# Splitting mixer weights ahead into DRAM, and moving scaling, halves and centring between engines, in a two-layer hybrid trunk

## Chip, cores and metric

One core of a Trainium2 chip runs the kernel. The metric is the device time of one execution in microseconds; lower is better. TensorE (PE in the profile) does the matmuls, VectorE (DVE), ScalarE (ACT) and GpSimd (POOL) the rest; SyncE (SP) issues the transfers. Inputs are float32, and the kernel works in float32 throughout, with products split in two parts as described below.

## What is computed

```python
def reference(x, ...):
    for layer in range(DEPTH):                       # 2 layers
        x = x + 0.5 * swiglu_ffn(x, ffn1_norm[layer], ffn1_w_in[layer], ffn1_w_out[layer])
        if layer % 2 == 0:
            x = x + retention_dilated_mixer(x, mix_norm[layer], hyb_w_in[e], ret_gn[e], hyb_w_out[e])
        else:
            x = x + stick_breaking_mixer(x, mix_norm[layer], sb_w_in[o], sb_w_out[o])
        x = x + 0.5 * swiglu_ffn(x, ffn2_norm[layer], ffn2_w_in[layer], ffn2_w_out[layer])
    return rms_norm(x, final_norm)
```

The sequence has 512 tokens, the model 1024 columns, the channel mixing 2816. `swiglu_ffn` is `(silu(h @ gate) * (h @ up)) @ w_out` on the RMS-normed `h`. The first mixer has 8 heads of 64 with retention (scores times a decay, a group norm per head, a swish gate) and 8 heads of dilated attention (a masked softmax). The second has 16 heads of stick-breaking attention: with z the score of a query and an earlier key, the weight is `exp(log_sigmoid(z) + sum over later keys of log_sigmoid(-z))`.

## The kernel before

Activations lie transposed: 8 chunks of 128 model columns by 512 tokens (`x`, and `hh` after the norm). Each float32 operand of a large product is split into a part `hi` (a rounded copy) and a part `lo` (the rest, by a subtract), and `mm3` (L138) sums three matmuls, hi by hi, hi by lo and lo by hi. `weight` (L121) does this for a weight tile of 128 by up to 1024: a load by SyncE into one of four `wraw` slots, `hi` by a ScalarE copy (L128) into `whi`, `lo` by a subtract (L129) into `wlo`, two slots each. The engine of L129 is in `lo_eng`: VectorE during the channel mixing, GpSimd during the two mixers (`lo_eng[0] = nc.gpsimd` at the foot of `trunk`).

The program runs in this order: `ffn` and `out_ffn` of layer 0, `hybrid`, `ffn` and `out_ffn` again, the same pair of layer 1, `stick`, `ffn` and `out_last`. `ffn` has 22 steps of two projection tiles (gate and up), each 8 chunks by three matmuls of 128 by 512. `out_ffn` has 8 steps of 66 matmuls.

`hybrid` first makes four gates (weights `hyb_g`). Then it works through eight pairs of heads, four of retention and four of dilated attention; `prep` of the next pair stands ahead of the core of the present one. `prep` projects values (`hyb_rv` or `hyb_dv`), then q and k through `qk_rot`: a shuffle (L441), three VectorE operations of the rotation (L443 to L445), and `pack_q` (ScalarE copies L399 and L400, VectorE rest L401) or `pack_k` (VectorE copy L381 and rest L382, twice each on 64 partitions). `retention_core` multiplies scores by the decay (L470), splits them (L146, L147), multiplies by the values (`attend`, L420, L425), then norms per head: a matmul with `bd` gives the mean (L477), VectorE subtracts it (L478), ScalarE squares (L480), a second matmul gives the variance (L482), and VectorE scales (L484, L486). `dilated_core` takes the mask and the minimum of each block of scores (L508), the exponents on ScalarE, a reciprocal (L511) and a scaling (L512) for each of the eight blocks, then transposes (L519) and goes on as above.

`stick_core` works on eight pairs, each head in three banks: scores, Abs (L593), Exp and Ln on ScalarE, L596 on VectorE, a split into `sp` (L151 and L152), the sums over later keys by matmuls with `tri` and `nones` (L617), an exponent, and a split into `ah`. `split_v` (L149) makes `hi` by a VectorE copy (L151) and `lo` by a subtract (L152) on the engine it is given: GpSimd for a pair's output, VectorE elsewhere. `out_mix` projects the eight outputs (`oa`, `ob` weights).

The program is written in this order, and a scheduler then sets each engine's own order by when buffers and operands come free; SyncE issues a load when its `wraw` slot is free. PSUM has eight banks: `acc` 3, `att` 4, `po` 1.

Of the kernel before, what the change touches and what calls it, by code (L numbers as in the profile page):

```python
# [34 lines left out]
def trunk(ctx: ExitStack, tc: tile.TileContext, a: dict, out: bass.AP):  # L35
# [113 lines left out]
    def split_v(hi, lo, src, eng=None):  # L149

        nc.vector.tensor_copy(out=hi, in_=src)  # L151
        (eng or nc.vector).tensor_tensor(out=lo, in0=src, in1=f32(hi), op=ALU.subtract)  # L152
# [223 lines left out]
    def pack_k(y):  # L376

        t = B((P, 2, SEQ), F32R, "qk")
        for e in range(2):
# [1 line left out]
            nc.vector.tensor_copy(out=t[own, e, :], in_=y[own, :])  # L381
# [113 lines left out]
    def dilated_core(p, q, k, v, dmask, outs):  # L495
        rows = {}
        for b in BANKS:
            ps = ATT()
# [4 lines left out]
            for e, i, at in QPARTS[b]:
                n = (i + 1) * P
                sl = slice(at, at + n)
                st = T((P, 4))

                nc.vector.tensor_tensor_reduce(out=s[:, sl], in0=ps[:, sl], in1=dmask[:, SEQ - n:], op0=ALU.add,  # L508
                                               op1=ALU.min, scale=1.0, scalar=3.0e38, accum_out=st[:, 0:1])
# [315 lines left out]
```

## Time and profile before

| | us |
|---|---|
| median of 3 runs | 2083.76 (2082.23 to 2086.93) |
| profiled execution, its own time | 2081.9 |
| its span | 2080.0 |
| mean granted TensorE clock | 0.992 of full speed |

| stage (part of the span, us) | TensorE busy | VectorE | ScalarE | GpSimd |
|---|---|---|---|---|
| channel mixing, 800 to 900 | 100.00 | 45.35 | 29.38 | 0.00 |
| hybrid, 360 to 700 | 302.55 of 340 | 251.40 | 150.93 | 104.63 |
| stick-breaking, 1400 to 1720 | 294.02 of 320 | 246.02 | 181.54 | 87.32 |

The first row is from a window of 100 us in a channel-mixing stage; the others contain the mixer and some of what stands beside it. An engine's time is busy time, which includes time in which an operation is under way and waits for something in it. The granted clock is that of TensorE. In the group rows the last column is the idle time ahead of a group on its engine, with what ended it; in the timeline rows it stands in brackets.

### The profile page before, as it was taken

To read this page: it belongs to the slowest core of one execution; us is meant where nothing else is said; L and a number is where in the kernel's file an instruction comes from. 1 tells how busy PE (TensorE), PEld (TensorE's weight loads), DVE (VectorE), ACT (ScalarE), POOL (GpSimd) and SP (SyncE) were. 2 spreads that over 40 slices of the span, in tenths; PEclk is the share of its full clock that TensorE was granted. 3 is DMA by queue.
4 is the path that set the end of the run, shared out by engine and by line. 5 is a ranking of instruction groups with operands and counts; after the bars stand their busy time and mean duration, and the time that the engine had idled before them with its cause. 6 is when DMAs were issued, how large, how long until landed. Compare 5 with 4: busy or idle time off the path is not lost.

```text
span 2080.0 us, 23646 instructions
## 1 busy us (share of the span) xinstructions
PE 1999.6 (96%) x9440; PEld 1662.7 (80%) x9440; DVE 1113.3 (54%) x1640; ACT 769.8 (37%) x1124; POOL 196.4 (9%) x104
## 2 busy tenths in 40 slices
PE   8999999987889999999999999999898999999997
PEld 7888888876667788888888888888777778888887
DVE  6444433378987644443344444336777874444334
ACT  5323332334445423233233323225655653232323
POOL 0000000532223000000000000003322220000000
PEclk9999999999999999999999999999999999999999
DMA  5223333312112332333332323332111032223333
GB/s 183 100 93 100 95 94 100 116 62 71 58 35 71 102 101 92 101 88 100 97 101 91 102 96 92 101 97 75 61 42 46 28 100 91 100 93 101 93 92 125
DMA packets 55695, 186.51 MB, mean 90 GB/s; under 512 B 6304, under 2 KB 7072, under 8 KB 55584
## 3 DMA queue, kind: packets, MB, share of 16 engines
q1 hardware_dynamic: 55584, 185.00, 28.0%
q8 instruction: 74, 1.21, 0.2%
q14 instruction: 37, 0.30, 0.0%
HBM read 182.88 MB, written 2.10 MB: 89 GB/s over the span
## 4 chain that ended last, share of the span: by engine, by line
PE 84%; DVE 12%; ACT 3%; issue 1%; DMA 0%; SPq 0%; DVEq 0%; ACTq 0%
PE acc L142 18%; PE acc L143 18%; PE acc L141 18%; PE att L141 8%; PE att L142 8%; PE att L143 8%; PE att L617 2%; PE po L420 2%; DVE qk L381 1%; ACT t L90 1%; DVE tp L444 1%; PE acc L345 1%; PE acc L344 1%; PE acc L343 1%; DVE qk L382 1%
## 5 line engine op out<-in xcount | busy, mean ns | idle before, releaser
L128 ACT CAST whi<-wraw 128x1024 fp32r<-128x1024 f32 (+3 forms) x352 | 356.3, 1012 | 1007.9 <-PE acc L142 550.4
L129 DVE TENSOR_TENSOR wlo<-wraw,whi 128x1024 fp32r<-128x1024 f32 (+1 forms) x276 | 328.5, 1190 | 238.9 <-ACT whi L128 236.9
L141 PE MATMUL acc<-h,whi 128*128 128x512 f32 x992 | 390.6, 394 | 6.0 <-ACT h L174 6.0
L142 PE MATMUL acc<-h,whi 128*128 128x512 f32 x992 | 389.8, 393 | 0.9 <-DVE h L175 0.6
L143 PE MATMUL acc<-h,wlo 128*128 128x512 f32 x992 | 390.0, 393 | 0.0
L129 POOL TENSOR_TENSOR wlo<-wraw,whi 128x1024 fp32r<-128x1024 f32 (+2 forms) x76 | 167.4, 2202 | 1436.6 <-ACT whi L128 1376.8
L141 PE MATMUL att<-h,whi 128*128 128x512 f32 x704 | 275.1, 391 | 0.0
L143 PE MATMUL att<-h,wlo 128*128 128x512 f32 x704 | 274.3, 390 | 0.0
L142 PE MATMUL att<-h,whi 128*128 128x512 f32 x704 | 273.9, 389 | 0.0
L141 PEld LDWEIGHTS acc<-h,whi 128*128 128x128 f32 x992 | 187.8, 189 | 44.9 <-ACT h L174 5.9
L142 PEld LDWEIGHTS acc<-h,whi 128*128 128x128 f32 x992 | 187.7, 189 | 41.1 <-DVE h L175 3.6
L143 PEld LDWEIGHTS acc<-h,wlo 128*128 128x128 f32 x992 | 187.6, 189 | 39.0 <-issue 0.7
L315 DVE TENSOR_TENSOR tp<-att,r 128x512 f32<-128x512 f32 x88 | 60.9, 692 | 281.4 <-PE att L143 281.4
L309 DVE TENSOR_TENSOR tp<-acc,r 128x512 f32<-128x512 f32 x88 | 60.9, 692 | 183.6 <-PE acc L143 183.4
L141 PEld LDWEIGHTS att<-h,whi 128*128 128x128 f32 x704 | 132.3, 188 | 28.0 <-issue 0.7
L142 PEld LDWEIGHTS att<-h,whi 128*128 128x128 f32 x704 | 132.0, 188 | 27.9 <-issue 0.7
L143 PEld LDWEIGHTS att<-h,wlo 128*128 128x128 f32 x704 | 132.1, 188 | 27.8 <-issue 0.2
L141 PE MATMUL acc<-o,whi 128*128 128x512 f32 (+1 forms) x352 | 135.3, 384 | 0.0
L142 PE MATMUL acc<-o,whi 128*128 128x512 f32 (+1 forms) x352 | 134.8, 383 | 0.0
L143 PE MATMUL acc<-o,wlo 128*128 128x512 f32 (+1 forms) x352 | 134.3, 382 | 0.0
L141 PEld LDWEIGHTS acc<-o,whi 128*128 128x128 f32 x352 | 66.5, 189 | 11.7
L142 PEld LDWEIGHTS acc<-o,whi 128*128 128x128 f32 x352 | 66.5, 189 | 11.7
(179 smaller groups left out, 2960.0 us busy)
## 6 DMA issues: line engine op xcount, KB each, us to landing
wraw<-f_in SPq DMA_DIRECT2D x174, 512.0 KB, 3.4
wraw<-f_out SPq DMA_DIRECT2D x68, 448.0 KB, 3.3
wraw<-f_out SPq DMA_DIRECT2D x34, 512.0 KB, 3.5
wraw<-sb_q SPq DMA_DIRECT2D x8, 512.0 KB, 3.4
wraw<-sb_k SPq DMA_DIRECT2D x8, 512.0 KB, 3.4
wraw<-sb_v SPq DMA_DIRECT2D x8, 512.0 KB, 3.4
wraw<-hyb_oa SPq DMA_DIRECT2D x8, 320.0 KB, 2.8
wraw<-sb_oa SPq DMA_DIRECT2D x8, 320.0 KB, 2.8
```

The source lines that it names most:

```text
L90: r = nc.scalar.activation(out=o, in_=i, func=f, **kw)
L128: nc.scalar.copy(out=hi[:, :cols], in_=raw[:, :cols])
L129: lo_eng[0].tensor_tensor(out=lo[:, :cols], in0=raw[:, :cols], in1=f32(hi[:, :cols]), op=ALU.subtract)
L141: nc.tensor.matmul(ps, h[:, col:col + P], rhs_hi, start=first, stop=False)
L142: nc.tensor.matmul(ps, h[:, col:col + P], rhs_lo, start=False, stop=False)
L143: nc.tensor.matmul(ps, l[:, col:col + P], rhs_hi, start=False, stop=last)
L309: nc.vector.tensor_mul(out=t1, in0=pg, in1=rr)
L315: nc.vector.tensor_mul(out=t2, in0=pu, in1=rr)
L343: nc.tensor.matmul(o, hi, wh, start=k == 0 and t % 2 == 0, stop=False, skip_group_check=True)
L344: nc.tensor.matmul(o, hi, wl, start=False, stop=False, skip_group_check=True)
L420: nc.tensor.matmul(po[:, SEQ - n:], st, banks[b][:, c, at:at + n], start=j == 0 and c == 0, stop=j == NB - 1 and c == 1, skip_group_check= ...
L617: nc.tensor.matmul(z[:, at + n - m:at + n], st, sp[:, c, s0:s0 + m], start=False, stop=i == len(adds) - 1 and c == 1, skip_group_check=True)
```

## The change

The weights of the mixers are split while a channel mixing runs and kept in DRAM. `cut_ahead` takes one unit (one weight tile) at a time: it calls `weight`, and writes `hi` and `lo` to a DRAM tile by two transfers. `ffn` calls it at the end of each step from the third on, `out_ffn` at the end of each step where it is given units. The hybrid mixer's 28 units of 1024 columns (`hyb_g`, values, q, k) are split in the first `ffn` (20) and `out_ffn` (8) of layer 0, the 36 stick-breaking units (with the output weights `sb_oa` and `sb_ob`) in the second `ffn` of layer 0 and the first of layer 1, 18 each. `weight_cut` later loads both halves: on odd turns one transfer of both into a `whl` slot, on even turns two transfers into two `wraw` slots. The hybrid mixer's output weights (`hyb_oa`, `hyb_ob`, 12 tiles) are still split where they are used, now by VectorE. `whi` and `wlo` (two slots each) become `whl` (three slots for both halves).

Besides, `pack_k`'s hi, the hi of the pairs' outputs and `r23`'s hi go from VectorE to ScalarE; the outputs' lo from GpSimd to VectorE. The group norm's first matmul takes `cd` (identity minus `bd`), so its result is already centred, and the subtract goes. The eight reciprocals per pair of dilated heads become two of 128 by 4, and the scaling goes to ScalarE, after all of a head's blocks. In `stick_core` the last loop takes the banks in the order bc, bb, ba.

```diff
-    whi = ctx.enter_context(tc.tile_pool(name="whi", bufs=2))
-    wlo = ctx.enter_context(tc.tile_pool(name="wlo", bufs=2))
+    whl = ctx.enter_context(tc.tile_pool(name="whl", bufs=3))
+    dram = ctx.enter_context(tc.tile_pool(name="dram", bufs=1, space=bass.MemoryType.DRAM))
...
+    def cut_ahead(key, cols):
+        src = a[key[0]]
+        for i in key[1:]:
+            src = src[i]
+        hi, lo = weight(src, cols)
+        keep = dram.tile([P, 2, cols], F32, tag="cut_" + "_".join(map(str, key)), name="cut_" + "_".join(map(str, key)))
+        for i, part in enumerate((hi, lo)):
+            nc.sync.dma_start(keep[:, i, :], f32(part[:, :cols]))
+        cut[key] = keep
+
+    def weight_cut(key, cols):
+        turns[0] += 1
+        keep = cut[key]
+        if turns[0] % 2:
+            hl = whl.tile([P, 2, 1024], F32R, tag="whl", name=nm("whl"))
+            nc.sync.dma_start(f32(hl[:, :, :cols]), keep)
+            return hl[:, 0, :], hl[:, 1, :]
+        hl = [wraw.tile([P, 1024], F32R, tag="wraw", name=nm("wcut")) for _ in range(2)]
+        for i in range(2):
+            nc.sync.dma_start(f32(hl[i][:, :cols]), keep[:, i, :])
+        return hl
+
+    def unit(key, cols):
+        if key in cut:
+            return weight_cut(key, cols)
...
     def out_ffn(w_out, us, gcol, ahead=None):
             norm_chunk(d, gcol, ss)
+            if ahead:
+                cut_ahead(*ahead.pop(0))
...
     def ffn(r, w_in, first=None, pieces=None, ahead=None):
             us.append(u)
+            if ahead and f > 1:
+                cut_ahead(*ahead.pop(0))
...
     def pack_k(y):
-            nc.vector.tensor_copy(out=t[own, e, :], in_=y[own, :])
+            nc.scalar.copy(out=t[own, e, :], in_=y[own, :])
...
     def retention_core(p, q, k, v, gate, outs, bd, cd):
-        mu = ATT()
-        nc.tensor.matmul(mu, bd, o, start=True, stop=True)
-        nc.vector.tensor_sub(out=o, in0=o, in1=mu)
+        cen = ATT()
+        nc.tensor.matmul(cen, cd, o, start=True, stop=True)
         sq = T()
-        nc.scalar.activation(out=sq, in_=o, func=AF.Square)
+        nc.scalar.activation(out=sq, in_=cen, func=AF.Square)
...
-        nc.vector.tensor_mul(out=o, in0=o, in1=rs)
+        nc.vector.tensor_mul(out=o, in0=cen, in1=rs)
-        split_v(oo[:, 0, :], oo[:, 1, :], o, nc.gpsimd)
+        split(oo[:, 0, :], oo[:, 1, :], o)
...
     def dilated_core(p, q, k, v, dmask, outs):
-                nc.vector.reciprocal(st[:, 2:3], st[:, 1:2])
-                nc.vector.tensor_scalar(s[:, sl], s[:, sl], st[:, 2:3], None, op0=ALU.mult)
+            if b[0] == "A":
+                nc.vector.reciprocal(st[:, 2, :], st[:, 1, :])
+                for i in range(NB):
+                    nc.scalar.activation(out=rows[e, i], in_=rows[e, i], func=AF.Copy, scale=st[:, 2, i:i + 1])
...
     def stick_core(p, q, k, v, cm, outs, idr, tri, nones):
-            split_v(r23[:, 0, :], r23[:, 1, :], t2, nc.vector)
+            split(r23[:, 0, :], r23[:, 1, :], t2)
-            for b in (bb, bc, ba):
+            for b in (bc, bb, ba):
...
-    lo_eng[0] = nc.gpsimd
     ss = hybrid(ss, 16)
-    lo_eng[0] = nc.vector
```

Three places show how instructions move. The first is SyncE's queue at the join of layer 0's first channel mixing and the hybrid mixer. Before, the last loads of the output projection are followed by the gates' weights and the tables:

```order
L127 DMA wraw_2458<-f_out 128x896
L127 DMA wraw_2492<-hyb_g 128x1024
...
L127 DMA wraw_2615<-hyb_g 128x1024
L450 DMA o_395_2651<-rot_ret 128x1024
L460 DMA o_435_2951<-decay 128x1024
```

Now there are the loads of the last units to be split, their writes (L150), and the loads of split weights (L161 both halves, L165 one half):

```order
L127 DMA wraw_2606<-f_out 128x896
L150 DMA cut_hyb_dq_2547<-whl_2543 128x1024 x2
L127 DMA wraw_2638<-hyb_dk 128x1024
L165 DMA wcut_2697<-cut_hyb_g_471 128x1024
...
L165 DMA wcut_2760<-cut_hyb_g_627 128x1024
L150 DMA cut_hyb_dk_2643<-whl_2639 128x1024 x2
...
L161 DMA whl_2647<-cut_hyb_g_393 128x2048
L161 DMA whl_2729<-cut_hyb_g_549 128x2048
```

The first gate's tile (`cut_hyb_g_393`) now stands behind the last unit's writes, and behind loads for the second and fourth gates.

The second place is a pair of the stick-breaking mixer, where k's projection (`acc`) has ended and the first scores (`att`) are to be turned into `sp`. VectorE before:

```order
L434 TENSOR_TENSOR tp_10457<-acc_10417,r_9851 128x512
L381 CAST qk_10459<-tp_10457 64x512 x2
L382 TENSOR_TENSOR qk_10459<-tp_10457,qk_10459 64x512 x2
L596 SCALAR_TENSOR_TENSOR t_10471<-att_10464,t_10471 128x512
L596 SCALAR_TENSOR_TENSOR t_10483<-att_10479,t_10483 128x256
L151 CAST sp_10476<-t_10471 128x512
```

VectorE now, at the same pair:

```order
L476 TENSOR_TENSOR tp_10588<-acc_10550,r_10006 128x512
L424 TENSOR_TENSOR qk_10590<-tp_10588,qk_10590 64x512 x2
L642 SCALAR_TENSOR_TENSOR t_10602<-att_10595,t_10602 128x512
L642 SCALAR_TENSOR_TENSOR t_10614<-att_10610,t_10614 128x256
L188 CAST sp_10607<-t_10602 128x512
```

The two copies of k have left VectorE. ScalarE before, from q's last copies on:

```order
L400 ACTIVATE qk_10450<-tp_10448 64x512
L128 CAST whi_10673<-wraw_10672 128x1024
L593 ACTIVATE t_10471<-att_10464 128x512
L593 ACTIVATE t_10483<-att_10479 128x256
L90 ACTIVATE t_10471<-t_10471 128x512
```

ScalarE now:

```order
L442 ACTIVATE qk_10581<-tp_10579 64x512
L423 CAST qk_10590<-tp_10588 64x512 x2
L639 ACTIVATE t_10602<-att_10595 128x512
L639 ACTIVATE t_10614<-att_10610 128x256
L90 ACTIVATE t_10602<-t_10602 128x512
```

A weight's copy has gone from the row, and k's two copies stand ahead of the Abs (L593, now L639).

The third place is ScalarE in a pair of dilated heads. Before, exponents (L90) alternate with the splits of transposed blocks, and the scaling between them is VectorE's:

```order
L90 ACTIVATE t_3980,t_3990<-t_3980,t_3990 128x128
L146 CAST ah_4018<-att_4013 128x512
L146 CAST c_663_4024<-att_4021 128x256
L90 ACTIVATE t_3996,t_3999<-t_3996,t_3999 128x256
L146 CAST ah_4032<-att_4027 128x512
L90 ACTIVATE t_4005,t_4008<-t_4005,t_4008 128x512
```

Now a head's four scalings (L558) stand between exponents, and the splits (L183) come later:

```order
L90 ACTIVATE t_4061,st_4062<-t_4061,st_4062 128x384
L558 ACTIVATE t_4033<-t_4033,st_4034 128x128
L558 ACTIVATE t_4044<-t_4044,st_4034 128x256
L558 ACTIVATE t_4033<-t_4033,st_4034 128x384
L558 ACTIVATE t_4050<-t_4050,st_4034 128x512
L90 ACTIVATE t_4061,st_4062<-t_4061,st_4062 128x128
L90 ACTIVATE t_4072,st_4062<-t_4072,st_4062 128x256
L90 ACTIVATE t_4078,st_4062<-t_4078,st_4062 128x512
L183 CAST ah_4093<-att_4088 128x512
```

The first head's scaling follows the second head's first exponent, and the split of the first transposed block waits behind all of the second head's exponents.

More of the change, by code (lines that the diff above doesn't have):

```diff
@@ L123, in weight @@
         raw = wraw.tile([P, 1024], F32, tag="wraw", name=nm("wraw"))
-        hi = whi.tile([P, 1024], F32R, tag="whi", name=nm("whi"))
-        lo = wlo.tile([P, 1024], F32R, tag="wlo", name=nm("wlo"))
+        hl = whl.tile([P, 2, 1024], F32R, tag="whl", name=nm("whl"))
+        hi, lo = hl[:, 0, :], hl[:, 1, :]
         if pieces is None:
@@ L137, in weight, with mm3 @@
         return hi, lo
-    def mm3(ps, whl, col, rhs_hi, rhs_lo, first, last):
-        h, l = whl
+    cut = {}
+    def cut_ahead(key, cols):
[7 more added lines that the diff above has]
+        cut[key] = keep
+    turns = [0]
+    def weight_cut(key, cols):
+        turns[0] += 1
+        keep = cut[key]
+        if turns[0] % 2:
+            hl = whl.tile([P, 2, 1024], F32R, tag="whl", name=nm("whl"))
+            nc.sync.dma_start(f32(hl[:, :, :cols]), keep)
[7 more added lines that the diff above has]
+            return weight_cut(key, cols)
+        src = a[key[0]]
+        for i in key[1:]:
+            src = src[i]
+        return weight(src, cols)
+    def mm3(ps, w, col, rhs_hi, rhs_lo, first, last):
+        h, l = w
         nc.tensor.matmul(ps, h[:, col:col + P], rhs_hi, start=first, stop=False)
@@ L197, in proj_tile @@
     def proj_tile(src, ps, w=None):
-        w = w or weight(src, D)
+        w = w or (unit(src, D) if isinstance(src, tuple) else weight(src, D))
         for k in range(KC):
@@ L283, in out_mix @@
             ps = ACC()
-            w = weight(wa[d], 640)
+            w = unit((wa, d), 640)
             for f in range(5):
@@ L289, in out_mix @@
             if d % 2 == 0:
-                w = weight(wb[d // 2], 768)
+                w = unit((wb, d // 2), 768)
             ps = ATT()
@@ L296, in out_mix, with ffn @@
         return ss
-    def ffn(r, w_in, first=None, pieces=None):
+    def ffn(r, w_in, first=None, pieces=None, ahead=None):
         us = []
@@ L335, in values @@
         for u in range(2):
-            h, l = weight(wsrc[u], 1024)
+            h, l = unit((*wsrc, u), 1024)
             for kk in range(4):
@@ L545, in hybrid @@
         bd = const("bd", P)
+        cd = const("cd", P)
         act_set(LNEXP)
@@ L684, in sums @@
         return norm_r(ss)
[L686 to L688 removed]
+    hyb = [(("hyb_g", p), D) for p in range(4)]
+    for n in "rd":
+        for p in range(4):
+            if p % 2 == 0:
+                hyb += [((f"hyb_{n}v", p // 2, u), D) for u in range(2)]
+            hyb += [((f"hyb_{n}q", p), D), ((f"hyb_{n}k", p), D)]
+    sb = []
+    for p in range(8):
+        sb += [(("sb_q", p), D), (("sb_k", p), D)]
+        if p % 2 == 0:
+            sb += [(("sb_v", p // 2, u), D) for u in range(2)]
+    sb += [(("sb_oa", d), 640) for d in range(8)] + [(("sb_ob", d), 768) for d in range(4)]
+    us = ffn(sums, a["f1_in"][0], first, [(c, c + 512, lambda: None) for c in (0, 512)], hyb)
+    ss = out_ffn(a["f1_out"][0], us, 8, hyb)
     ss = hybrid(ss, 16)
[L690 to L691 removed]
+    half = sb[:18]
+    us = ffn(lambda: norm_r(ss), a["f2_in"][0], ahead=half)
     ss = out_ffn(a["f2_out"][0], us, 24)
[L693 removed]
+    half = sb[18:]
+    us = ffn(lambda: norm_r(ss), a["f1_in"][1], ahead=half)
     ss = out_ffn(a["f1_out"][1], us, 32)
[L695 removed]
     ss = stick(ss, 40)
[L697 removed]
     us = ffn(lambda: norm_r(ss), a["f2_in"][1])
```

54 lines of the change are left out of this document (25 added, 29 removed).

## Prediction

> **What bounds the kernel now.** I read the page's busy line and its chain first, then windows of the trace by stage, then, inside the stages where TensorE waits, the groups by line with what ended the idle time before them, and last the rows in order of time around the longest waits.
>
> ```profile
> PE 1999.6 (96%) x9440; PEld 1662.7 (80%) x9440; DVE 1113.3 (54%) x1640; ACT 769.8 (37%) x1124; POOL 196.4 (9%) x104
> PE 84%; DVE 12%; ACT 3%; issue 1%; DMA 0%; SPq 0%; DVEq 0%; ACTq 0%
> ```
>
> TensorE is busy 96% of the span, and the matmuls' number does not change. But the chain that ended last spends 15% on VectorE and ScalarE, so there are places where they are late. The windows (columns: length, then busy time and count of each engine, granted clock, DMA share, GB/s) say where:
>
> ```profile
> 800.00:900.00 100.00, 100.00 (x442) 82.79 (x442) 45.35 (x54) 29.38 (x36) 0.00 (x0) 1.00 0.31 100
> 360.00:700.00 340.00, 302.55 (x1536) 250.79 (x1535) 251.40 (x456) 150.93 (x266) 104.63 (x52) 0.96 0.22 72
> 1400.00:1720.00 320.00, 294.02 (x1614) 246.89 (x1614) 246.02 (x444) 181.54 (x321) 87.32 (x44) 1.00 0.18 59
> ```
>
> In the channel mixing (800 to 900) TensorE never waits: nothing that shortens VectorE or ScalarE is worth anything there. In the retention and dilated mixer (360 to 700, "hybrid") it waits 340.00 − 302.55 = 37.4 us, in the stick-breaking mixer (1400 to 1720) 320.00 − 294.02 = 26.0 us. These 63.4 us are what the change can reach, and of the three windows only these two have GpSimd (the fifth engine column) at work. What ended the waits (last column of the groups by line; TensorE, hybrid first, then stick-breaking):
>
> ```profile
> L409 PE MATMUL att<-qk,qk 128*128 128x256 f32 x16 | 6.2, 386 | 25.0 <-DVE t L470 17.4 <-DVE t L508 7.3 <-DVE ah L147 0.3
> L409 PE MATMUL att<-qk,qk 128*128 128x384 f32 x16 | 6.7, 418 | 3.9 <-DVE t L165 3.9
> L420 PE MATMUL po<-ah,v 128*128 128x512 f32 x32 | 12.7, 433 | 3.9 <-DVE t L425 3.0 <-DVE ah L147 0.8
> L519 PE MATMUL att<-ident,t 128*128 128x128 f32 x80 | 13.1, 280 | 3.1 <-DVE t L512 1.9 <-DVE ah L147 1.1
> ...
> L617 PE MATMUL att<-sp,tri 128*128 128x384 f32 x32 | 12.9, 403 | 18.6 <-DVE sp L151 17.4 <-DVE sp L152 1.1
> L420 PE MATMUL po<-ah,v 128*128 128x512 f32 x32 | 14.6, 455 | 3.9 <-DVE t L425 2.6 <-DVE ah L151 1.0
> L617 PE MATMUL att<-sp,tri 128*128 128x512 f32 x32 | 13.0, 408 | 1.5 <-DVE sp L151 1.5
> ```
>
> Every wait ends with VectorE, which is busy only 251.40 of 340 us there. The rows in order of time show why it is late. VectorE, GpSimd and TensorE before the longest wait:
>
> ```profile
> 411.28 2.65 DVE L444 TENSOR_TENSOR tp<-tp,o 128x512 f32<-128x512 f32 x1
> 418.77 2.61 DVE L444 TENSOR_TENSOR tp<-tp,o 128x512 f32<-128x512 f32 x1
> 422.14 2.95 DVE L381 CAST qk<-tp 64x512 fp32r<-64x512 f32 x2
> 427.84 0.68 DVE L444 TENSOR_TENSOR tp<-tp,o 128x512 f32<-128x512 f32 x1
> 431.96 0.73 DVE L441 STREAM_SHUFFLE tp<-acc 128x512 f32<-128x512 f32 x1
> 433.33 2.55 DVE L444 TENSOR_TENSOR tp<-tp,o 128x512 f32<-128x512 f32 x1
> 435.81 0.55 DVE L470 TENSOR_TENSOR t<-att,o 128x384 f32<-128x384 f32 x1
> 437.08 0.86 DVE L381 CAST qk<-tp 64x512 fp32r<-64x512 f32 x2
> 433.00 2.34 POOL L129 TENSOR_TENSOR wlo<-wraw,whi 128x1024 fp32r<-128x1024 f32 x1 [8.64 <-ACT whi L128]
> 437.21 0.58 PE L409 MATMUL att<-qk,qk 128*128 128x256 f32 x1 [7.74 <-DVE t L470]
> ```
>
> The same L444 takes 0.68 us at 427.84 and 2.55 us at 433.33; the second stands beside a GpSimd subtract (433.00 to 435.34) and ends just behind it. The long ones at 411, 418 and 422 read alike. Their excess is 1.97 + 1.93 + 2.09 + 1.87 = 7.86 us, and TensorE's wait at 437.21 is 7.74 us. So the weights' subtracts on GpSimd (L129) hold up VectorE, and VectorE holds up TensorE.
>
> **The change part by part.**
>
> *GpSimd's subtracts go.* Their count and what they cost VectorE, by line (busy, mean ns):
>
> ```profile
> L129 POOL TENSOR_TENSOR wlo<-wraw,whi 128x1024 fp32r<-128x1024 f32 x52 | 126.7, 2436 | 1326.8 <-ACT whi L128 1295.5 <-issue 24.6 <-PE po L420 6.7
> L444 DVE TENSOR_TENSOR tp<-tp,o 128x512 f32<-128x512 f32 x8 | 14.7, 1839 | 0.0
> L444 DVE TENSOR_TENSOR tp<-tp,misc 128x512 f32<-128x512 f32 x8 | 10.7, 1343 | 0.1
> L147 DVE TENSOR_TENSOR ah<-t,ah 128x512 fp32r<-128x512 f32 x16 | 15.6, 978 | 1.8 <-ACT ah L146 1.6
> L445 DVE TENSOR_TENSOR tp<-tp,tp 128x512 f32<-128x512 f32 x16 | 14.3, 893 | 0.3
> ...
> L381 DVE CAST qk<-tp 64x512 fp32r<-64x512 f32 x16 | 20.2, 1265 | 0.5
> L401 DVE SCALAR_TENSOR_TENSOR qlo<-tp,qk 64x512 fp32r<-64x512 f32 x16 | 18.1, 1129 | 3.2 <-ACT qk L399 3.0
> ```
>
> Against 0.68 us undisturbed, hybrid loses 8 × 1.16 + 8 × 0.66 + 16 × 0.30 + 16 × 0.21 = 22.7 us in four groups. In stick-breaking, L381 loses 16 × (1.265 − 0.43) = 13.4 us (0.43 is half of the pair at 437.08) and L401 16 × 0.45 = 7.2 us. With no subtract left on GpSimd between these stages' ends, I take all of it off VectorE. What TensorE gets of it:
>
> - Retention, the 17.4 us ended by L470. At the first such wait the whole 7.86 us goes, but the new order still sets a wait: behind the end of k's projection, VectorE runs the shuffle (0.73 at 431.96), two multiplies (0.68 each) and the first L470 (0.55 at 435.81), 2.6 us, about 2.4 us of it uncovered. In the next two pairs the previous group norm's steps stand in between on VectorE, and q's four copies on ScalarE stand ahead of the square: my walk through the rows gives 3.8 and 2.5. An estimate of 8.7 us stays, **8.7 go**.
> - Dilated, 7.3 (L508) + 3.1 (L519) + 3.9 (L420) = 14.3 us. The scaling leaves VectorE, and eight reciprocals become two; but ScalarE now carries exponents and scaling in one row. I let 5 us stay, **9.3 go**. The 3.9 us ended by L165 are the norm at the head of a stage; they stay.
> - The clock. Behind long waits the granted clock falls:
>
> ```profile
> 430.00:440.00 10.00, 2.79 (x13) 2.79 (x14) 9.20 (x14) 3.48 (x5) 2.34 (x1) 0.60 0.15 52
> 470.00:480.00 10.00, 4.49 (x12) 3.69 (x13) 9.81 (x17) 2.84 (x5) 2.34 (x1) 0.66 0.16 52
> ```
>
>   Over the hybrid window it is 0.96, so 13.6 us of clock are missing, much of it while TensorE was idle anyway. Without the waits of 6 us and more I take back **6 us** (between 0 and 10).
> - Group norm. The centring subtract leaves VectorE (4 × 0.68 = 2.7 us by L444's size) for a matmul that was there already as the mean's; it lies in a chain that other heads partly cover: **2 us** (0 to 2.7).
> - Stick-breaking. Here k's hi moves to ScalarE, ahead of the chain Abs, Exp, Ln:
>
> ```profile
> L400 ACT ACTIVATE qk<-tp 64x512 fp32r<-64x512 f32 x16 | 10.1, 631 | 0.4
> L593 ACT ACTIVATE t<-att 128x512 f32<-128x512 f32 x32 | 19.4, 607 | 0.8 <-PE att L589 0.8
> 1475.34 2.97 DVE L381 CAST qk<-tp 64x512 fp32r<-64x512 f32 x2
> 1481.19 0.44 PE L617 MATMUL att<-sp,tri 128*128 128x384 f32 x1 [2.50 <-DVE sp L151]
> ```
>
>   Undisturbed, the pair on VectorE would be 0.86 us; on ScalarE it is an estimated 2 × 0.63 = 1.26 us by L400, and it delays L593 and what follows by as much. From the end of k's projection to the first hi of sp is 6.6 us now; with the copies in front and no blocking I get 5.9 in one kind of iteration and 5.25 in the other, so 1.07 us less on average: 7.5 us over seven iterations of the 18.6. The short waits (1.5 and 1.0 at L617, 3.9 at L420) lose perhaps 5, and matmuls that are spaced a little wide beside them 1.5. **14 us go** (8 to 24).
>
> *Weights are split ahead.* 64 units are loaded, split and written to DRAM in steps of the channel mixing. ScalarE and VectorE spend 64 × (1.05 + 1.22) us more there:
>
> ```profile
> L128 ACT CAST whi<-wraw 128x1024 fp32r<-128x1024 f32 x31 | 32.6, 1050 | 41.0 <-issue 18.1 <-PE acc L142 15.3 <-POOL wlo L129 6.4
> L129 DVE TENSOR_TENSOR wlo<-wraw,whi 128x1024 fp32r<-128x1024 f32 x34 | 41.6, 1223 | 25.4 <-ACT whi L128 25.4
> ```
>
> One step there is 48 matmuls, 48 × 100/442 = 10.86 us; VectorE is busy 45% of it and would be 57%, ScalarE 29% and 39%. That is covered by TensorE. The DMA is the open part: a step moved 100 GB/s × 10.86 us = about 1 MB, and now 2.5 MB (half a megabyte more read, one written, and the split weights' share of tiles as before), about 240 GB/s.
>
> ```profile
> 8.00:20.00 12.00, 12.00 (x45) 9.36 (x44) 11.54 (x18) 9.15 (x16) 0.00 (x0) 1.00 0.83 315
> wraw<-f_in SPq DMA_DIRECT2D x174, 512.0 KB, 3.4
> outT<-c SPq DMA_DIRECT2D x3, 256.0 KB, 2.0
> ```
>
> The start of the kernel reads 315 GB/s for 12 us with TensorE full, so 240 fits on average. Order matters more: on SyncE's queue the writes of a unit wait for its split, and the next step's two loads stand behind them. The slot of the next up tile comes free when those writes have landed. Walked through with 3.4 us for a load and up to 4 us for a written half, the writes land about 7 us into the step and the up tile is ready at 9.4 us, where it is needed after three tiles of 24 matmuls, at 16.3 us. Cost taken: 0 (bounds 0 and 96, the rival below).
>
> By the Trainium skill (HBM Reference, Specifications (TRN2)) one core's effective share of the memory is about 358 GB/s; 240 is under it, while the trace has 315 for reads and nothing of reads mixed with writes.
>
> *The first loads of the mixers.* Split weights are 1 MB a tile instead of 0.5. The first gate's tile is issued behind the last unit's writes, its slot is released by a tile that ends not quite one projection (24 matmuls, 5.4 us) before its first use, and about 1.5 MB is queued ahead: at 315 GB/s this is 4.8 us, and its own 1 MB 3.3, 8.1 in all, of which a part has gone by at the release. I charge **2 us** (0 to 5). The 12 projections of the output that keep splitting in place put 12 subtracts on VectorE, beside matmuls that have no wait.
>
> Sum: 8.7 + 9.3 + 6 + 2 + 14 − 2 = 38 us. The profiled execution took 2081.9 us, 1.9 over its span and 1.9 under the median of the runs, so the forecast is 2081.9 − 38 = **2044 us**.
>
> **The rivals.**
>
> *Nearly all waits go.* If my walks keep too much, what stays is the norm's 3.9 us and a little at the joins: 37.4 − 5.4 + 26.0 − 5 + 8 of clock − 2 = 59, thus **2023**. For it: the excess of 7.86 matches the wait of 7.74 almost fully. Against: VectorE and ScalarE still form a serial row behind each k.
>
> By the Trainium skill (SBUF — State Buffer, SBUF: two separate sides) VectorE and GpSimd share one port pair, locked for a whole instruction, and no other pair of engines contends; VectorE operations with two SBUF inputs then lose all of their excess here. The row at 433.33 agrees, ending 0.54 us behind GpSimd's.
>
> *ScalarE becomes the wait.* k's copies ahead of L593, the scaling behind the exponents and the square behind q's copies, each on the path: 8 × 2 × 0.63 = 10 us in stick-breaking, and in the dilated part half of 32 scalings of some 0.5 us (L400 has 0.63 for 512 columns), 8 us, eat what VectorE gives: 38 − 18 = 20, thus **2062**. For it: the copies that move are slower on ScalarE than undisturbed on VectorE (0.63 against 0.43). Against: ScalarE is busy 181.54 of 320 us.
>
> *The channel mixing stalls (slower).* If reads and writes in one queue take so long that an up tile comes late, each of the 64 steps pays. It decides from 7 us of delay a step, by which time the written tile's slot is given back too late; from there on 1 us costs 64. Loads and writes one at a time would be 3 × 3.4 + 2 × 4 = 18 us against a step of 10.86. At 1.5 us a step: 2044 + 96 = **2140**. Against: landings overlap, or 315 GB/s could not be in the trace.
>
> *The change does not do it.* If GpSimd is only a bystander and the long rows come from something else, only the moved operations count, some 3 us either way: **2080**.
>
> **How the numbers follow.** Forecast (2034 to 2056) 0.50; nearly all waits go 0.17; ScalarE 0.20; no effect 0.04; stalls 0.07; the rest lies at the edges. The range's low end is all 63.4 us and 8 of clock less the 2 at the joint, 2012; its high end is ScalarE's case with 4 us less of clock, 2066. It leaves out the stalls, no effect and the end of the ScalarE case. A measurement of this kernel can tell about 0.2% (4 us) from no change: faster 0.89, within 0.04, slower 0.07.
>
> **What would show it.** Right: no GpSimd subtract; the rotation's second multiply (L444, then L486) at 0.68 us everywhere and k's hi off VectorE in both mixers; TensorE's idle time near 18 us in hybrid and 14 in stick-breaking; the clock at 0.60 gone at the first head pair; TensorE still full in the channel mixing at a DMA share near 0.7. Wrong: TensorE's idle time ahead of L141 in layer 0's first channel mixing, released by a weight; ScalarE named as the releaser of most waits in the mixers; or VectorE operations that stay at over 1 us with GpSimd empty.

## The result, and the profile after

| | before | after |
|---|---|---|
| median of 4 runs each, us | 2082.99 (2082.05 to 2086.93) | 2018.35 (2017.89 to 2020.19) |
| profiled execution, its span | 2081.9, 2080.0 | 2018.12, 2016.3 |
| ratio of the runs, 95% interval | | 0.969 (0.967 to 0.971) |

The changed kernel is 65 us faster; the forecast was 38. The time lies in the range given (2012 to 2066 us), but below the band of 2034 to 2056 that had half of the chance. The page of the changed kernel, its busy line and its chain:

```profile
PE 1987.0 (99%) x9440; PEld 1656.3 (82%) x9440; DVE 1092.6 (54%) x1608; ACT 812.5 (40%) x1220; POOL 7.3 (0%) x12
PE 94%; DVE 3%; ACT 2%; issue 1%; DMA 0%; DVEq 0%; SPq 0%; ACTq 0%
```

TensorE is at 99% in place of 96%, and VectorE and ScalarE have 5% of the chain in place of 15%. VectorE's share of busy time is 54% as before, but the time has moved: the rows below have it 49 and 39 us less busy in the two mixers, and 32 us more in the first channel mixing, which now splits weights ahead. To see where the time went, the trace is cut at the matmuls that sum the norms (`ones_ms`), which stand at the same place of both programs to within a few matmuls. The rows of windows (length first, then busy time of TensorE, weight loads, VectorE, ScalarE, GpSimd, granted clock, DMA share, GB/s) of the kernel before, for layer 0's first channel mixing (with the first gate's tile at its end), the hybrid mixer, and the stick-breaking mixer:

```profile
19.91:374.76 354.85, 354.85 (x1565) 293.47 (x1564) 153.29 (x179) 108.02 (x131) 4.79 (x2) 1.00 0.33 103
374.76:686.90 312.14, 274.69 (x1416) 228.06 (x1414) 238.63 (x441) 139.78 (x253) 99.84 (x50) 0.96 0.21 67
1412.30:1710.31 298.01, 272.03 (x1520) 229.02 (x1518) 235.32 (x432) 172.44 (x311) 82.35 (x41) 1.00 0.18 57
```

and of the changed kernel:

```profile
19.71:376.74 357.03, 355.17 (x1564) 293.39 (x1564) 185.25 (x207) 131.22 (x156) 0.00 (x0) 1.00 0.68 231
376.74:644.12 267.38, 264.12 (x1420) 221.32 (x1418) 189.47 (x378) 140.61 (x283) 5.03 (x4) 1.00 0.37 127
1368.54:1648.48 279.94, 270.94 (x1519) 230.26 (x1518) 196.40 (x401) 165.98 (x318) 0.00 (x0) 1.00 0.32 110
```

The hybrid mixer is 44.8 us shorter, the stick-breaking mixer 18.1; the first channel mixing is 2.2 us longer. In hybrid, TensorE waits 267.38 − 264.12 = 3.3 us where it waited 37.5, and its busy time is 10.6 us shorter for the same matmuls, since the granted clock is 1.00 in place of 0.96. The two norm intervals between the mixers are 1.0 and 0.0 us shorter, and the last channel mixing's end 2. In the kernel before, a tile there waited for a weight's subtract:

```profile
2061.80 0.38 PE L143 MATMUL acc<-qk,wlo 128*128 128x256 f32 x1 [1.87 <-DVE wlo L129]
```

The changed kernel has no such row. What TensorE still waits for, by line, hybrid and then stick-breaking:

```profile
L178 PE MATMUL acc<-h,whl 128*128 128x512 f32 x120 | 47.7, 398 | 1.9 <-DMA whl<-cut_hyb_g 1.9
L451 PE MATMUL att<-qk,qk 128*128 128x256 f32 x16 | 5.6, 352 | 2.6 <-DVE st L551 1.7 <-DVE t L512 0.8
...
L663 PE MATMUL att<-sp,tri 128*128 128x384 f32 x32 | 12.1, 379 | 3.5 <-DVE sp L188 3.5
L663 PE MATMUL att<-sp,nones 128*128 128x128 f32 x32 | 8.7, 288 | 4.8 <-DVE sp L188 4.8
```

The 25.0 us ahead of the 256-wide scores have become 2.6. At the place of the longest wait, 7.74 us, there is now this (the two parts of a timeline, VectorE then TensorE):

```profile
428.94 0.69 DVE L485 TENSOR_TENSOR tp<-acc,o 128x512 f32<-128x512 f32 x1
429.55 0.68 DVE L486 TENSOR_TENSOR tp<-tp,o 128x512 f32<-128x512 f32 x1
430.14 0.55 DVE L512 TENSOR_TENSOR t<-att,o 128x384 f32<-128x384 f32 x1
429.68 0.33 PE L385 MATMUL acc<-whl,h 128*128 128x256 f32 x1
431.55 0.38 PE L451 MATMUL att<-qk,qk 128*128 128x256 f32 x1 [0.34 <-DVE t L512]
```

The rotation's second multiply takes 0.68 us, and TensorE waits 0.34 us. Between its scores and this wait it has matmuls of the values (L385 from 429.68 on) to do. The granted clock, which fell to 0.60 and 0.66 behind the long waits of the kernel before, is 1.00 over the whole mixer.

### The profile page after: what moved, and what is told of

It reads as the page before. It is cut to its first block, busy times and chain, and to the rows that moved or that the text cites. A ratio compares the mean times of both kernels' runs of the same rounds, so it can differ in the third digit from the quotient of the medians.

```text
span 2016.3 us, 23888 instructions
## 1 busy us (share of the span) xinstructions
PE 1987.0 (99%) x9440; PEld 1656.3 (82%) x9440; DVE 1092.6 (54%) x1608; ACT 812.5 (40%) x1220; POOL 7.3 (0%) x12
## 4 chain that ended last, share of the span: by engine, by line
PE 94%; DVE 3%; ACT 2%; issue 1%; DMA 0%; DVEq 0%; SPq 0%; ACTq 0%
PE acc L179 20%; PE acc L178 20%; PE acc L180 20%; PE att L179 8%; PE att L178 8%; PE att L180 8%; PE att L663 2%; PE po L462 2%; PE acc L387 1%; PE acc L385 1%; PE acc L386 1%; PE att L451 1%; ACT t L90 1%; ACT qk L423 0%; PE att L564 0%
## 5 line engine op out<-in xcount | busy, mean ns | idle before, releaser
L128 ACT CAST whl<-wraw 128x1024 fp32r<-128x1024 f32 (+3 forms) x352 | 354.9, 1010 | 862.2 <-PE acc L180 488.7
L129 DVE TENSOR_TENSOR whl<-wraw,whl 128x1024 fp32r<-128x1024 f32 (+3 forms) x352 | 411.8, 1173 | 273.5 <-ACT whl L128 272.8
L178 PE MATMUL acc<-h,whl 128*128 128x512 f32 x848 | 332.5, 392 | 7.7 <-ACT h L211 5.8
L179 PE MATMUL acc<-h,whl 128*128 128x512 f32 x848 | 332.0, 391 | 0.0
L180 PE MATMUL acc<-h,whl 128*128 128x512 f32 x848 | 331.7, 391 | 0.0
L178 PE MATMUL att<-h,whl 128*128 128x512 f32 x704 | 274.7, 390 | 0.0
L180 PE MATMUL att<-h,whl 128*128 128x512 f32 x704 | 274.3, 390 | 0.0
L179 PE MATMUL att<-h,whl 128*128 128x512 f32 x704 | 274.3, 390 | 0.0
L178 PEld LDWEIGHTS acc<-h,whl 128*128 128x128 f32 x848 | 160.1, 189 | 41.1 <-ACT h L211 5.8
L179 PEld LDWEIGHTS acc<-h,whl 128*128 128x128 f32 x848 | 159.8, 188 | 33.0 <-DVE h L212 1.0
L180 PEld LDWEIGHTS acc<-h,whl 128*128 128x128 f32 x848 | 159.7, 188 | 32.9 <-issue 0.2
L179 PEld LDWEIGHTS att<-h,whl 128*128 128x128 f32 x704 | 132.3, 188 | 28.2 <-issue 0.7
L180 PEld LDWEIGHTS att<-h,whl 128*128 128x128 f32 x704 | 132.2, 188 | 27.8 <-issue 0.5
L178 PEld LDWEIGHTS att<-h,whl 128*128 128x128 f32 x704 | 132.0, 187 | 27.9 <-issue 0.5
L178 PE MATMUL acc<-o,whl 128*128 128x512 f32 (+1 forms) x332 | 126.9, 382 | 0.0
L179 PE MATMUL acc<-o,whl 128*128 128x512 f32 (+1 forms) x332 | 126.3, 380 | 0.0
L180 PE MATMUL acc<-o,whl 128*128 128x512 f32 (+1 forms) x332 | 126.3, 380 | 0.0
L180 PEld LDWEIGHTS acc<-o,whl 128*128 128x128 f32 x332 | 62.5, 188 | 11.3
L179 PEld LDWEIGHTS acc<-o,whl 128*128 128x128 f32 x332 | 62.5, 188 | 11.2
L178 PEld LDWEIGHTS acc<-o,whl 128*128 128x128 f32 x332 | 62.5, 188 | 11.2
```

Source lines behind the costliest of these rows:

```text
L128: nc.scalar.copy(out=hi[:, :cols], in_=raw[:, :cols])
L129: lo_eng[0].tensor_tensor(out=lo[:, :cols], in0=raw[:, :cols], in1=f32(hi[:, :cols]), op=ALU.subtract)
L178: nc.tensor.matmul(ps, h[:, col:col + P], rhs_hi, start=first, stop=False)
L179: nc.tensor.matmul(ps, h[:, col:col + P], rhs_lo, start=False, stop=False)
L180: nc.tensor.matmul(ps, l[:, col:col + P], rhs_hi, start=False, stop=last)
```

## The experiments

Theory 1: GpSimd's weight subtracts held up VectorE's operations, and nearly the whole gain is that they are gone. Theory 2: a large share comes from the operations that were moved or dropped. Each interval below is read from windows cut at the norm matmuls as above. The experiments ran on three chips, on which the kernel before had medians of 2084.86, 2083.43 and 2084.60 us; the changed kernel has only the time above, so differences of a microsecond or two from 2018.35 are read from the stages, not from the time alone.

**Only splitting ahead** (b_cut): the changed kernel with the other edits undone.

```diff
-            nc.scalar.copy(out=t[own, e, :], in_=y[own, :])
+            nc.vector.tensor_copy(out=t[own, e, :], in_=y[own, :])
...
-        split(oo[:, 0, :], oo[:, 1, :], o)
+        split_v(oo[:, 0, :], oo[:, 1, :], o, nc.gpsimd)
```

(and so on for the scaling, the centring, `r23` and the order of the sums)

> Only the weights are split ahead (and the weight slots changed); k's hi, the scaling, the centring, the outputs' halves and the order of sums are as before. Theory 1, GpSimd's weight subtracts held VectorE up and hardly anything else counts: 2020 to 2032 us, the hybrid part between its two norm matmuls at 268 to 278 us against 312 before and 267 after the change; the rest to the changed kernel is the 16 output subtracts still on GpSimd. Theory 2, the moved operations give a large share: 2040 us or more, hybrid at 290 us or more.

Measured 2021.70 us, ratio 0.970 (0.968 to 0.972).

```profile
378.46:652.21 273.75, 265.09 (x1420) 222.09 (x1419) 210.75 (x454) 114.20 (x227) 16.40 (x12) 1.00 0.36 124
1376.64:1653.70 277.06, 269.97 (x1520) 229.52 (x1518) 202.30 (x433) 145.52 (x278) 10.29 (x8) 1.00 0.33 111
```

Splitting ahead alone brings all but about 3 us of the gain. Hybrid is 6.4 us longer than in the changed kernel, but stick-breaking is 2.9 us shorter: there the other edits cost something. The single edits undone below change hybrid by 0.7, 0.5 and 0.1 us; what makes up the rest, the outputs' lo on GpSimd among the candidates, was not run alone.

**All but splitting ahead** (c_rest): weights split in place, lo on GpSimd in the mixers.

```diff
+    lo_eng[0] = nc.gpsimd
     ss = hybrid(ss, 16)
+    lo_eng[0] = nc.vector
```

(the same about `stick`, and no unit is split ahead)

> All of the change but the splitting ahead: the mixers' weights are loaded and split where they are used, lo on GpSimd. Theory 1: 2060 to 2078 us, with the rotation's second multiply still at 1.3 to 1.9 us on average. Theory 2: 2045 us or less.

Measured 2073.56 us, ratio 0.994 (0.993 to 0.996). The rotation's second multiply is still held up; VectorE's groups in hybrid:

```profile
L486 DVE TENSOR_TENSOR tp<-tp,o 128x512 f32<-128x512 f32 x8 | 17.6, 2201 | 0.0
L486 DVE TENSOR_TENSOR tp<-tp,misc 128x512 f32<-128x512 f32 x8 | 13.3, 1659 | 0.0
```

The other edits alone are worth some 11 us. They take VectorE work out of the mixers, but what is left meets the subtracts as before (2201 and 1659 ns where 680 would do; 13 of the 16 multiplies start while a subtract is under way). Theory 1 holds on both sides. The profiled run, the slowest of five at 2078.60 us, does not tell how the 11 us lie over the stages: hybrid took 304.73 us, but stick-breaking 306.23, at a granted clock of 0.97 and with TensorE idle for 25.1 us as before (26.0).

**GpSimd put back to work** (g_sub): values unchanged, one operation more for each unit that comes from DRAM.

```diff
+    def again(lo, cols):
+        nc.gpsimd.tensor_tensor(out=lo[:, :cols], in0=f32(lo[:, :cols]), in1=zero.to_broadcast([P, cols]), op=ALU.subtract)
...
+            again(hl[:, 1, :], cols)
...
+        again(hl[1], cols)
```

> The changed kernel, with one more GpSimd operation for each of the 64 units that come back from DRAM: lo minus zero, in place, which reads and writes SBUF (about 2.4 us each); values are unchanged. Theory 1: most of the loss returns, 2045 to 2085 us, and VectorE's operations with two SBUF operands lengthen beside them. Theory 2: 2018 to 2028 us, as nothing was put back on VectorE or ScalarE.

Measured 2053.96 us, ratio 0.985 (0.983 to 0.987). 36 us come back, with VectorE's and ScalarE's programs unchanged. GpSimd's first group, then VectorE's in hybrid:

```profile
L158 POOL TENSOR_TENSOR wcut<-wcut,zero 128x1024 fp32r<-128x1024 f32 x26 | 51.0, 1960 | 1285.8 <-DMA wcut<-cut_sb_k 825.4 <-DMA wcut<-cut_hyb_g 355.4 <-DMA wcut<-cut_hyb_dk 35.8
L432 DVE TENSOR_TENSOR qk<-tp,qk 64x512 fp32r<-64x512 f32 x16 | 15.8, 985 | 1.5 <-ACT qk L431 1.1
L494 DVE TENSOR_TENSOR tp<-tp,o 128x512 f32<-128x512 f32 x8 | 7.4, 924 | 0.0
L494 DVE TENSOR_TENSOR tp<-tp,misc 128x512 f32<-128x512 f32 x8 | 5.5, 682 | 0.0
L493 DVE TENSOR_TENSOR tp<-acc,o 128x512 f32<-128x512 f32 x8 | 5.5, 682 | 0.1
```

Operations with two SBUF operands lengthen (985 and 924 ns); L493, with one operand in PSUM, keeps 682. Stick-breaking is back at 299.1 us, hybrid only at 279.8 of 312. TensorE's waits in the mixers still end with VectorE; for the added operation itself it waits 0.9 us in all.

Hybrid gets less back for two reasons. GpSimd has 28 operations of 51.3 us there, where the kernel before had 50 of 99.8 us. And the rotation's second multiply meets them late. In the retention pairs six of its eight start while a GpSimd operation is under way, as six did in the kernel before, but mostly near its end, as these rows show; in the dilated pairs none does, where four did.

```profile
417.94 2.43 POOL L158 TENSOR_TENSOR whl<-whl,zero 128x1024 fp32r<-128x1024 f32 x1 [3.28 <-DMA whl<-cut_hyb_rq]
420.04 0.88 DVE L494 TENSOR_TENSOR tp<-tp,o 128x512 f32<-128x512 f32 x1
```

This multiply starts 0.33 us ahead of the GpSimd operation's end (420.37) and ends 0.55 us behind it. The one at 433.33 in the kernel before starts 0.33 us behind the subtract's start and also ends 0.54 us behind its end. So what such a meeting costs VectorE is about what is left of the GpSimd operation when VectorE's starts.

**GpSimd busy, but reading nothing** (g_mem): memsets over a unit's slots ahead of its load.

```diff
+            nc.gpsimd.memset(f32(hl[:, :, :cols]), 0.0)
             nc.sync.dma_start(f32(hl[:, :, :cols]), keep)
...
+        for i in range(2):
+            nc.gpsimd.memset(f32(hl[i][:, :cols]), 0.0)
```

> The changed kernel, with GpSimd memsets over the slots of each unit ahead of its load from DRAM (about 2 us for a unit), so GpSimd is as busy as before but reads nothing. If what blocks is a GpSimd operation that reads SBUF: 2018 to 2024 us, the rotation's multiplies stay at 0.68 us; copies from SBUF to SBUF on VectorE may lengthen. If any busy GpSimd blocks: 2045 us or more, with long multiplies.

Measured 2021.67 us, ratio 0.970 (0.968 to 0.972). Hybrid is at 267.7 us against 267.4, with these groups of GpSimd and VectorE:

```profile
L161 POOL MEMSET whl<- 128x2048 f32 x26 | 47.2, 1817 | 149.2 <-PE acc L183 95.0 <-PE acc L390 54.3
L489 DVE TENSOR_TENSOR tp<-tp,o 128x512 f32<-128x512 f32 x8 | 5.4, 680 | 0.0
```

GpSimd has 111 us of memsets in all its groups of them, and VectorE's operations with two SBUF operands do not notice. They do meet: six of the eight multiplies of the retention pairs start while a memset is under way, as here.

```profile
424.76 1.81 POOL L161 MEMSET whl<- 128x2048 f32 x1 [3.81 <-PE acc L183]
426.13 0.68 DVE L489 TENSOR_TENSOR tp<-tp,o 128x512 f32<-128x512 f32 x1
```

Of the 3.3 us lost, 0.7 are in stick-breaking and 2.0 in the first interval, at the join (359.07 us against 357.03). Those 2.0 need not come from the memsets: b_cut and e_scale, which have none, took 358.62 and 358.88 us there. In all three runs the granted clock fell behind TensorE's wait for the first gate's load, and in the changed kernel's it did not (windows at the join, changed kernel and then e_scale):

```profile
365.00:385.00 20.00, 18.14 (x79) 14.08 (x78) 5.62 (x9) 4.83 (x7) 3.40 (x3) 1.00 0.77 285
365.00:385.00 20.00, 17.86 (x71) 13.79 (x70) 4.93 (x8) 4.19 (x6) 0.91 (x1) 0.91 0.79 287
```

So it is not GpSimd's being busy but its reading of SBUF that holds such operations up. By the Trainium skill (SBUF — State Buffer, SBUF: two separate sides) a VectorE operation with two SBUF inputs contends only against a GpSimd operation that reads SBUF; these two runs agree.

**The subtracts on VectorE, in place** (a_dve), in the kernel before, at both mixers:

```diff
-    lo_eng[0] = nc.gpsimd
```

> The kernel before, with the mixers' weights split in place as before but lo subtracted on VectorE in place of GpSimd. Theory 1: a blocked operation costs VectorE 1.9 us for a subtract of 2.4 us, the subtract itself 1.22 us, so most of the loss goes without any splitting ahead: 2035 to 2060 us, VectorE's rotation at 0.68 us. Theory 2, VectorE's load is what counts and not the blocking: 2080 us or more, since VectorE gains 64 us of work.

Measured 2055.60 us, ratio 0.986 (0.985 to 0.988).

```profile
375.03:676.26 301.23, 279.35 (x1418) 229.49 (x1417) 240.28 (x479) 139.39 (x253) 19.03 (x12) 0.95 0.22 69
1400.90:1686.45 285.55, 272.71 (x1522) 231.12 (x1521) 237.34 (x465) 171.54 (x311) 11.16 (x8) 0.99 0.18 58
```

Of the 76 subtracts that move, 40 are for hybrid's weights. VectorE's busy time there stays about where it was (240.28 against 238.63), since the held-up time is gone, and the kernel is 29 us faster than the 2084.60 of the same chip. TensorE still waits 21.9 us in hybrid. The other 37 us to the changed kernel come only with the splitting out of the mixers.

**k's hi back on VectorE** (d_khi).

```diff
-            nc.scalar.copy(out=t[own, e, :], in_=y[own, :])
+            nc.vector.tensor_copy(out=t[own, e, :], in_=y[own, :])
```

> The changed kernel with k's hi back on VectorE. Theory 1: without GpSimd's subtracts the pair of copies takes 0.86 us on VectorE and leaves ScalarE free for the Abs as soon as the scores are there, so the eight waits of 1.3 us in stick-breaking shrink: stick-breaking 270 to 276 us between its norm matmuls against 279.9, hybrid 267 to 271; total 2009 to 2016 us. Theory 2, VectorE is the bound and the move to ScalarE was worth it: 2019 us or more, stick-breaking at 280 or more.

Measured 2014.75 us, against 2018.35 for the change. Stick-breaking takes 275.70 us (279.94), hybrid 268.05 (267.38). The end of a pair's first scores on TensorE and ScalarE's rows behind it, in the changed kernel, and then ScalarE's here:

```profile
1488.96 0.39 PE L635 MATMUL att<-cmask,idr 128*128 128x128 f32 x2
1489.37 1.26 ACT L423 CAST qk<-tp 64x512 fp32r<-64x512 f32 x2 [2.86 <-DVE tp L476]
1490.66 0.87 ACT L639 ACTIVATE t<-att 128x512 f32<-128x512 f32 x2
```

```profile
1488.61 0.87 ACT L639 ACTIVATE t<-att 128x512 f32<-128x512 f32 x2 [2.87 <-PE att L635]
```

In the changed kernel ScalarE idles 2.86 us for k's product, copies for 1.26 us, and only then takes the Abs, whose first scores were complete at about 1489.4, when the copies began. Without the copies the Abs waits for the scores alone.

**The scaling back on VectorE** (e_scale) and **the centring subtract back** (f_norm).

```diff
-            if b[0] == "A":
-                nc.vector.reciprocal(st[:, 2, :], st[:, 1, :])
-                for i in range(NB):
-                    nc.scalar.activation(out=rows[e, i], in_=rows[e, i], func=AF.Copy, scale=st[:, 2, i:i + 1])
+                nc.vector.reciprocal(st[:, 2, i:i + 1], st[:, 1, i:i + 1])
+                nc.vector.tensor_scalar(s[:, sl], s[:, sl], st[:, 2, i:i + 1], None, op0=ALU.mult)
```

```diff
-        nc.tensor.matmul(cen, cd, o, start=True, stop=True)
+        nc.tensor.matmul(mu, bd, o, start=True, stop=True)
+        nc.vector.tensor_sub(out=o, in0=o, in1=mu)
```

> The changed kernel with eight reciprocals and the scaling on VectorE as before. Theory 1, little is left to gain there: 2016 to 2022 us, hybrid 266 to 271. Theory 2, the scaling was a main term (9 us by the prediction, with the rest of the dilated part): 2023 us or more.

> The changed kernel with the mean by a matmul and the centring subtract on VectorE as before. Predicted term 2 us: 2018 to 2022 us, hybrid 267 to 271. If the chain of the group norm sets the pace without GpSimd: 2023 or more.

Measured 2019.62 and 2018.74 us; hybrid 267.89 and 267.44 against 267.38. Neither edit is worth anything that these runs can tell once GpSimd is quiet.

**The first gate split in place** (h_gate).

```diff
-    hyb = [(("hyb_g", p), D) for p in range(4)]
+    hyb = [(("hyb_g", p), D) for p in range(1, 4)]
```

> The changed kernel with the first gate's weight not split ahead but loaded and split where it is used; 27 units are split ahead in place of 28. If the 2.2 us at the join come from its load queued behind other transfers: 2015.5 to 2017, and the first interval back at 354.9 us from 357.0. If they come from anything else of the DMA traffic: 2018 and 357.

Measured 2015.42 us; the first interval is 354.84 us, with TensorE busy throughout. The edit also halves that load (the raw weight in place of both parts), so it does not tell its size from its place in the queue. In the changed kernel TensorE waits at the join for the first gate's load, which SyncE issues behind the last unit's writes (timelines of TensorE and of SyncE's queue):

```profile
371.12 0.50 PE L178 MATMUL acc<-h,whl 128*128 128x512 f32 x1 [1.86 <-DMA whl<-cut_hyb_g]
360.91 1.58 SPq L150 DMA_DIRECT2D cut_hyb_dk<-whl  x2
364.54 1.42 SPq L161 DMA_DIRECT2D whl<-cut_hyb_g  x2
```

**Each unit written twice** (i_twice), to see how near the channel mixing is to stalling.

```diff
...
+            nc.sync.dma_start(more[:, i, :], f32(part[:, :cols]))
```

> The changed kernel, with every unit written to DRAM a second time beside the channel mixing (1 MB more a step, about 3.5 MB per 10.86 us, some 330 GB/s if nothing waits). If the channel mixing has the 7 us of reserve of the prediction's walk: 2018 to 2024 us and 359 us for the intervals with units as now. If it is near its limit: 1 to 3 us a step, 2080 to 2200 us, with TensorE waiting for weights there.

Measured 2021.89 us, ratio 0.970 (0.968 to 0.971). A window inside the channel mixing:

```profile
100.00:230.00 130.00, 130.00 (x575) 107.63 (x574) 73.69 (x84) 50.98 (x60) 0.00 (x0) 1.00 0.89 332
```

The DMA engines are busy 0.89 at 332 GB/s, and TensorE does not wait. The changed kernel has 0.71 and 241 GB/s in the same window. Of the 3.5 us lost, 2.4 are at the join (359.48 us): TensorE waits 2.75 us there in place of 1.86, and the clock falls behind it as in e_scale (0.91).

**Three slots before** (j_three), in the kernel before:

```diff
-    whi = ctx.enter_context(tc.tile_pool(name="whi", bufs=2))
-    wlo = ctx.enter_context(tc.tile_pool(name="wlo", bufs=2))
+    whi = ctx.enter_context(tc.tile_pool(name="whi", bufs=3))
+    wlo = ctx.enter_context(tc.tile_pool(name="wlo", bufs=3))
```

> The kernel before, with three slots each for the weights' hi and lo, as the changed kernel has. If the 2 us that the last channel mixing's end lost come from the third slot: 2080 to 2083 us, the interval of 10.5 us between the last norm matmuls at 8.3, all else within 1 us. If the third slot also matters in the mixers: below 2078.

Measured 2084.79 us (2077.47 to 2090.63), ratio 1.000 (0.998 to 1.001), above the range expected. The interval at the end is 8.34 us in place of 10.46, so the third slot is what saved 2 us there. In its profiled run stick-breaking took 303.25 us against 298.01:

```profile
1412.88:1716.13 303.25, 277.88 (x1524) 235.22 (x1522) 235.37 (x433) 172.63 (x310) 79.61 (x40) 0.98 0.18 56
```

TensorE's idle time is 25.4 us there, as before (26.0); the difference is in its busy time, at a granted clock of 0.98 in place of 1.00. Runs of both kernels spread over 9 to 13 us, and the time goes with the clock: of the 17 runs of the kernel before on this chip, the two fastest (2080.41 and 2081.06 us) had 0.994, the two slowest (2089.14 and 2089.35) 0.988. Why the clock differs from run to run is open.

**A combination** (best): the first gate in place, k's hi on VectorE in stick-breaking alone, and the first bank's Abs, Exp and Ln ahead of the second's.

```diff
...
+                if b == bc:
+                    tc.add_manual_dep(ab.ins, last.ins.name, nosync, reason="bank by bank")
```

> The changed kernel with the first gate's weight split in place, k's hi back on VectorE in stick-breaking alone, and there on ScalarE the first bank's Abs, Exp and Ln ahead of the second bank's. The first two give 2015.4 - 4.2 = 2011 if they add; the third brings the first sp about 0.7 us earlier in eight waits, so 2005 to 2009 us. If ScalarE's pass over the first bank costs as much later: 2011 or more.

Measured 2016.70 us, worse than either of its first two parts alone. Hybrid and the join are as expected (266.96 and 354.85), but stick-breaking took 282.32 us. VectorE there:

```profile
1487.82 1.41 DVE L424 TENSOR_TENSOR qk<-tp,qk 64x512 fp32r<-64x512 f32 x2
1489.26 0.69 DVE L644 SCALAR_TENSOR_TENSOR t<-att,t 128x512 f32<-128x512 f32 x1
1491.05 0.42 DVE L644 SCALAR_TENSOR_TENSOR t<-att,t 128x256 f32<-128x256 f32 x1
```

ScalarE now has the first bank ready before VectorE has done k's lo (L424), so the earlier bank gains little, and the second bank's part comes 1.8 us behind the first. I read this as the cause; it was not tested further, and it covers only part. Against d_khi's stick-breaking, 2.3 of the 6.6 us are longer waits (8.0 in place of 5.7), and 4.3 are busy time of TensorE, at the same clock of 1.00. The first two parts without the third, some 2011 us if they add, were not run.

## Why the prediction was right, and what it got too small

- *What bounds.* Right: TensorE's waits in the two mixers, caused by GpSimd's subtracts. Undoing everything else left 2021.7 us; bringing the GpSimd operations back alone cost 36 us; GpSimd operations that read nothing cost at most 3.
- *Retention, 8.7 us said to stay.* This is the step that failed. The row of waits for L512 is 0.8 us. At the first pair I counted VectorE's 2.6 us behind k's projection as nearly uncovered, but TensorE has its scores and matmuls of the values there (427.90 to 431.21), which left 0.34 us. The 3.8 and 2.5 us of the next pairs are gone too. Taking away the subtracts does this nearly alone: b_cut has 2.5 us of these waits left, c_rest 14.8 of 17.4. That VectorE and ScalarE reach those places earlier with nothing held up ahead is my reading, not shown by a run of its own.
- *The 3.9 us ended by L165, said to stay.* I took them for the norm at the head of a stage. They stand in the group norms of two retention pairs, the first of them here:

```profile
500.34 0.69 PE L409 MATMUL att<-qk,qk 128*128 128x384 f32 x1 [2.09 <-DVE t L165]
```

  The multiply ahead of it took 2.21 us from 495.00 on, beside a subtract (494.28 to 496.66), so I read this wait too as the subtracts' doing. In the changed kernel 0.4 us are left, with splitting ahead alone (b_cut) 0.2, and with the subtracts kept (c_rest) 2.4.
- *Dilated, 5 us to stay.* The wait for L551 is 1.7 us; those ahead of the transposes and of the values' matmuls are 0.2 or less. That ScalarE's scaling or the reciprocals mattered was wrong: undoing them changed hybrid by 0.5 us. The group norm's 2 us were 0.1.
- *The clock, 6 us.* Undersized: at 0.96 the same matmuls took 10.6 us more of busy time than at 1.00. The hybrid term was 26 us in all and came to 44.8.
- *Stick-breaking, 14 us.* It is 18.1. The copies ahead of the Abs were priced in the right place (the 1.07 us a pair comes to 1.03 from the three figures beside it); with k's hi on VectorE it would have been 22.3.
- *The join, 2 us.* Measured 2.2, at the load named; gone in h_gate.
- *The channel mixing, 0.* Right: TensorE busy 130.00 of 130 us even with each unit written twice, so the slower rival had more reserve than my walk gave it.
- *Missed:* the third weight slot, 2 us at the end.

Of the rivals, "nearly all waits go" (2023 us) came nearest to the 2018. The evidence for it stood in the prediction: an excess of 7.86 us beside a wait of 7.74. "ScalarE becomes the wait" was true only of k's copies in stick-breaking, at 4.2 us.

## What to carry to other kernels

Before moving work to GpSimd, look at what VectorE does beside it: an operation that looks free on an idle engine cost this kernel more than the same subtract on VectorE (29 us by a_dve), because it lengthens VectorE's operations with two SBUF operands (and its copies within SBUF). Where rows of one operation have two durations, subtract the short one and compare the excess with the wait downstream; if they match, forecast that the wait goes, and keep a remainder only where TensorE is seen to have no matmul left to fill it. A transfer that is only bandwidth can hide under a full TensorE up to 332 GB/s here; what showed was the first gate's load, issued behind writes at the join of two stages.
